# Value chunks that make their operand sums in place, half by half, with their weights loaded one quarter per step

## The chip, the cores and the metric

The kernel runs on one core of one Trainium2 chip. The core has five engines that run their own instruction streams: TensorE (PE in the profile; its weight loads are PEld), VectorE (DVE), ScalarE (ACT), GpSimd (POOL) and SyncE (SP). Each engine takes its instructions strictly in order; an instruction waits until what it reads is there and what it overwrites has been read. Transfers (DMA) between the chip's main memory and the on-chip memory are issued as instructions of SP or of ACT (rows SPq and ACTq) and then run on 16 DMA engines beside the compute engines.

The metric is the device time of one execution in microseconds, the median of the runs shown. The profile is of one execution.

## The reference, cut to what matters

The reference is one layer of a streaming encoder on 2048 rows of 1024 numbers. The rows are normed and multiplied by one wide weight matrix, whose columns are then split into queries, keys, values and gates of two branches and two mixing gates:

```python
IN_SPLITS = (A_WIDTH, A_WIDTH, A_WIDTH, A_WIDTH, R_QK_WIDTH, R_QK_WIDTH, R_V_WIDTH, R_V_WIDTH, D_MODEL, D_MODEL)
...
h = rms_norm(x, norm_gain[l])
proj = jnp.einsum('bsd,df->bsf', h, w_in[l])
q_a, k_a, v_a, g_a, q_r, k_r, v_r, g_r, m_a, m_r = split_columns(proj)
```

Branch A is attention over the own chunk of 64 rows and the eight before it, branch B a retention with a decaying state and a rotation of its queries and keys. Both are gated, projected, mixed and added to the input, and the sum is normed. The change concerns the projection `proj` alone, and of it the columns of the values `v_a` (512 columns) and `v_r` (1024 columns).

## The kernel before, in words

**Numbers.** All products are kept near fp32: an operand is split into a high part in fp32r (a cast by ScalarE, `wh`) and a low part, the rest (a subtraction by VectorE, `wl`), and a product is made of three matmuls: high by high, high by low, low by high.

**Strassen's scheme.** The big products are made in seven products of half-size blocks in place of eight. The seven left operands stay on the chip (the tiles `R[m]`, high and low). The right operands come from the weights of a chunk, four quarters b11, b12, b21, b22, and four sums made by GpSimd: t1 = b12 - b11, t2 = b22 - t1, t3 = b12 - b22, t4 = b21 - t2. The seven products use b11, t2, t3, b21, t1, t4 and b22 (the list `PRODUCTS`: left operand, right operand, PSUM bank).

**Chunks and steps.** The work of TensorE is one long list `seq` of items, walked by the generator `dense`. A projection job `p0` (rows 0 to 1023) or `p1` (rows 1024 to 2047) has eleven chunks: query, key, rotated key, value A, rotated query, first value B, key, rotated key, query, rotated query, second value B. Then come the gate jobs `g0`, `g1`, whose items are also used to fill TensorE during the attention and retention stages. An ordinary chunk (`Strassen`) has 256 columns and seven items of twelve matmuls with 512 columns each. A value chunk (class `Rows`: chunks 3, 5 and 10 of `p0` and `p1`) has 512 columns, and its result comes out with rows on the partitions. It has fourteen items, each of the seven products in two halves kk of the contraction, and its two halves of rows are two `Side` objects with their own PSUM banks. It takes its products in the order "g": b11, t2, b21, t3, t1, t4, b22.

**What sets the order.** The kernel writes the order of every engine by hand. While TensorE's item `at` is emitted, `prime` prepares the operand of item `at + 3` (`ahead[0]` is 3): `prepare` issues ScalarE's cast, and VectorE's low part is issued four steps later (`soon(LO_LAG, ...)`; an item is four steps). GpSimd's sums for an item are issued one preparation earlier still (`ch.sums`, called by `prime` for the item after the next one). For a value chunk, both halves of t1 and of t2 are issued together ahead of its first item's preparation, t3 and t4 ahead of the item that uses them. Evacuations of PSUM, stores and table loads are deferred by `later` and `put` to a later step, each on its engine's queue.

**Loads.** Weights are loaded by ScalarE's queue (`act.dma_start`). The dictionary `sooner` in `dense` says at which item a chunk's loads are issued: a lead of 9 and of 8 items before its first item (`RAW_LEADS`). The chunk behind a value chunk isn't loaded by these leads: at the value chunk's first item, `dense` sees that the following chunk has no weights yet and loads them then. An ordinary chunk has two tiles of 512 KB in a ring of three (tag "raw"). A value chunk loads b11 and b12 into two tiles of that ring at lead 9, and b21 and b22 as four transfers of 256 KB at lead 8 into four tiles of the general pool.

**Tiles.** The general pool of a projection phase (`E`, tag "e") has `E_PROJ` = 23 tiles of 2 KB per partition: casts and tables and results on their way to memory. A value chunk takes six of them: b21 and b22 in halves, and t2 in halves. Its t1 takes two of the three tiles of tag "t", t3 overwrites b12 and t4 overwrites b21.

**Start.** `start_up` norms and turns the first 1024 rows and makes the left operands of `p0` while the first two chunks (`Front`) run with plain products. It uses tiles of the general pool for x, for the turned blocks a11, a12 and a21, for the sum s3, and for two quarters of the second chunk's weights; s2 overwrites a11.

In the trace, buffer numbers are left out: `raw_p` are loaded quarters of `p0` and `p1` (also in the general pool, and after t3 or t4 has overwritten them), `t_p` are t1 to t4 in own tiles, `wh_p` and `wl_p` the high and low parts, `ps_p_x` to `ps_p_z` the PSUM banks. Nearly every instruction has line 142, the helper that records the order.

Of the kernel before, what the change touches and what calls it, by code (L numbers as in the profile page):

```python
# [11 lines left out]
F32 = mybir.dt.float32  # L12
# [4 lines left out]
ALU = mybir.AluOpType  # L17
# [4 lines left out]
P = 128  # L22
# [8 lines left out]
T = 256  # L31
# [12 lines left out]
ORDERS = {"p": (0, 4, 1, 2, 3, 5, 6), "g": (0, 1, 3, 2, 4, 5, 6)}  # L44
# [6 lines left out]
RAWS = 3  # L51
SUMS = 3
LO_LAG = 4
CS = 6
E_PROJ = 23
E_ATT = 16
E_RET = 22
E_MRG = 23
# [4 lines left out]
ROT_LATE = 10  # L63
PUT = 6
RAW_LEADS = (9, 8)
TR_LATER = 16
YR_0 = (2, 10, 1)
YR_1 = (102, 15, 2)
# [4 lines left out]
def hybrid_kernel(  # L73
# [23 lines left out]
    wp = ctx.enter_context(tc.tile_pool(name="wp", bufs=1))  # L97
# [4 lines left out]
    epool, xpool = [None], [None]  # L102

    def r32(ap):
        return ap.bitcast(F32)
# [7 lines left out]
    def E(name, dt=F32, shape=(P, 512)):  # L113
        return epool[0].tile(list(shape), dt, tag="e", name=name)
# [37 lines left out]
    pe, act, dve, pool = Ordered(nc.tensor), Sometimes(nc.scalar), Sometimes(nc.vector), Sometimes(nc.gpsimd)  # L152
# [107 lines left out]
    def soon(n, fn):  # L260

        later(n, fn) if ahead[0] else fn()
# [6 lines left out]
    class Chunk:  # L269
# [7 lines left out]
        def load(self, js=None):  # L277
            self.raw = self.raw or []
            for j in range(self.job.kh) if js is None else js:
                raw = wp.tile([P, 4, T], F32, tag="raw", bufs=RAWS, name=f"raw_{self.job.name}_{self.c}_{j}")  # L280
                (dma if self.job.resident else act.dma_start)(raw, self.job.stream(self.c, j))
                self.raw.append(raw)
# [36 lines left out]
    SUMS_OF = (("t1", "b12", "b11"), ("t2", "b22", "t1"), ("t3", "b12", "b22"), ("t4", "b21", "t2"))  # L319
# [14 lines left out]
    class Strassen(Chunk):  # L334
        tag = ""
# [32 lines left out]
        def prepare(self, n):  # L368
            self.sums(n)
            for s in SUMS_OF:  # L370
                if s[0] == PRODUCTS[n][1]:
                    self.sum(*s)
            late = pool if n in self.job.lo_pool else dve
            self.make(n, self.b[PRODUCTS[n][1]], late)
# [51 lines left out]
    class Rows(Strassen):  # L426
# [6 lines left out]

        def load(self, js=None):
            self.raw = self.raw or []
            for j in range(2) if js is None else js:
                for h in range(2):
                    src = w_cols(w_in, self.job.cols[self.c] + T * h, 2, j)
                    name = f"raw_{self.job.name}_{self.c}_{j}{h}"
                    if j == 0:  # L440
                        raw = wp.tile([P, 4, T], F32, tag="raw", bufs=RAWS, name=name)
                        act.dma_start(raw, src)
                        bs = [raw[:, 2 * kk:2 * kk + 2] for kk in range(2)]
                    else:
                        bs = [E(f"{name}_{kk}", shape=(P, 2, T)) for kk in range(2)]
                        for kk in range(2):
                            act.dma_start(bs[kk], src[:, 2 * kk:2 * kk + 2])
                    self.b[f"b{j + 1}{h + 1}"] = bs
                self.raw.append(j)

        def made(self, dst, one, two, into=None):
            if dst in self.b:
                return
            name = f"{dst}_{self.job.name}_{self.c}"
            if into:
                ts = self.b[into]
            elif dst == "t1":
                ts = [
                    wp.tile([P, 4, P], F32, tag="t", bufs=SUMS, name=f"{name}_{kk}")
                    .rearrange("p k c -> p (k c)").rearrange("p (k c) -> p k c", k=2)  # L460
                    for kk in range(2)
                ]
            else:
                ts = [E(f"{name}_{kk}", shape=(P, 2, T)) for kk in range(2)]
            for kk in range(2):
                pool.tensor_tensor(ts[kk], self.b[one][kk], self.b[two][kk], ALU.subtract)
            self.b[dst] = ts

        def sums(self, at):
            n, kk = at  # L470
            if kk:
                return
            if n == 0:
                self.made("t1", "b12", "b11")
                self.made("t2", "b22", "t1")
            elif n == 3:
                self.made("t3", "b12", "b22", "b12")
            elif n == 4:
                self.made("t4", "b21", "t2", "b21")

        def prepare(self, at):
            self.sums(at)
            n, kk = at
            src = self.b[PRODUCTS[n][1]][kk]
            name = f"{self.job.name}_{self.c}_{n}_{kk}"
            wh, wl = (
                wp.tile([P, 4, P], F32R, tag="p", bufs=PARTS, name=f"w{i}_{name}")
                .rearrange("p k c -> p (k c)").rearrange("p (k c) -> p k c", k=2)
                for i in "hl"
            )  # L490
            act.copy(wh, src)
            soon(LO_LAG, lambda: dve.tensor_tensor(wl, src, r32(wh), ALU.subtract))
            self.parts[at] = wh, wl

        def product(self, at):
            n, kk = at
# [120 lines left out]
    def dense(jobs):  # L617
        chunks = [ch for job in jobs for ch in job.chunks]
        following = dict(zip(chunks, chunks[1:]))
        starts = [k for k, (job, ch, n) in enumerate(seq) if isinstance(ch, Plain) and ch.at(n)[2] == 0]  # L620
        count, begins = {}, {}
        for at, (job, ch, n) in enumerate(seq):
            if isinstance(ch, Strassen):
                begins.setdefault(ch, at)
        sooner = {at - lead: (ch, [j]) for ch, at in begins.items() for j, lead in enumerate(RAW_LEADS)}
        one, two_, three = jobs[2].chunks[:3]
        for ch in (one, two_, three):
            for lead in RAW_LEADS:
                sooner.pop(begins[ch] - lead)
        two_.raw, three.raw = [], []  # L630
        at = begins[one]
        sooner[at - 9], sooner[at - 6] = (one, [0]), (one, [1])

        first_out = jobs[-1].chunks[0]
        at = begins[first_out]
        for lead in RAW_LEADS:
            sooner.pop(at - lead)
        sooner[at - 8], sooner[at - 5] = (first_out, [0]), (first_out, [1])
        operands = {begins[ch] - 2: ch for ch in begins if ch.job.before}
        for at, (job, ch, n) in enumerate(seq):  # L640
            free[0] = job.name[0] == "g"
            count[ch] = count.get(ch, 0) + 1
            if at in sooner:
                ch2, js = sooner[at]
                if ch2.raw is None or js[0]:
                    len(ch2.raw or ()) == js[0] and ch2.load(js)
            if count[ch] == job.when + 1 and ch in following and following[ch].raw is None:
                following[ch].load()
            prime(at + ahead[0] + 1)
            while starts and starts[0] <= at + job.lead:  # L650
                _, ch2, n2 = seq[starts.pop(0)]
                ch2.before(n2)
            if at in operands:
                operands[at].before()
            for _ in ch.product(n):
                yield True
                free[0] = job.name[0] == "g"
            for fn in hooks.get((job.name, ch.c, n), ()):
                fn()
            yield True  # L660
# [33 lines left out]
    def start_up():  # L694
# [3 lines left out]
        ch = jobs[0].chunks[:2]  # L698
# [5 lines left out]
        left, right = slice(0, P), slice(P, T)  # L704
# [45 lines left out]
                R[m][1][:, k, :], ps, ng[:, g:g + 1], r32(R[m][0][:, k, :]), ALU.mult, ALU.subtract  # L750
            )

        for i in range(2):
            ch[1].b[f"b2{i + 1}"] = E(f"b2{i + 1}", shape=(P, 4, P))
        for t in range(4):
            rows(xa, 0, t)
        for c in range(2):
# [32 lines left out]
        a11 = [E(f"a11_{k}") for k in range(4)]  # L790
# [14 lines left out]
        a12 = [E(f"a12_{k}") for k in range(4)]  # L805
# [16 lines left out]
                run_to(28)  # L822
        run_to(32)
        a21 = [E(f"a21_{k}") for k in range(4)]
        s3 = [E(f"s3_{k}") for k in range(4)]
        for k in range(4):
            act.activation(a21[k], ps[k], AF.Copy, scale=ng[:, k:k + 1])
            dve.scalar_tensor_tensor(s3[k], ps[k], ng[:, k:k + 1], a11[k], ALU.mult, ALU.subtract)
# [6 lines left out]
            hi(2, k, ps[k], 4 + k)  # L835
            lo(2, k, ps[k], 4 + k)
        run_to(48)
        s2, s1, s4 = a11, a21, a12
        for k in range(4):
            dve.scalar_tensor_tensor(s2[k], ps[k], ng[:, 4 + k:5 + k], s3[k], ALU.mult, ALU.add)  # L840
            pool.tensor_tensor(s4[k], a12[k], s2[k], ALU.subtract)
# [119 lines left out]
    def w_cols(w, col, n, j):  # L961
        rows = w.shape[1] // n
        return w[0, rows * j:rows * j + rows, col:col + T].rearrange("(k p) f -> p k f", p=P)
# [855 lines left out]

    st = open_phase("proj0", E_PROJ, 4)  # L1820
    jobs = [
# [15 lines left out]
    end, at = {}, 0  # L1837
# [65 lines left out]

    run_to(end["p0"] + TR_LATER + 4)
    flush()
# [6 lines left out]

    st = open_phase("proj1", E_PROJ, 4)
    ch = jobs[2].chunks[1]
    ch.b = {}
    for key in ("b11", "b12", "b21", "b22"):
        ch.b[key] = E(f"{key}_p1", shape=(P, 4, P))
        j, h = int(key[1]) - 1, int(key[2]) - 1
        dma(ch.b[key], w_cols(w_in, jobs[2].cols[1], 2, j)[:, :, h * P:(h + 1) * P])
    run_to(end["g0"])  # L1920
    for h in range(HEADS):
        later(10 + 44 * h, lambda h=h: finish_yr(h, 0, None, 18))
    run_to(end["p1"] + TR_LATER + 4)
    flush()
# [77 lines left out]
```

## Time and profile before

| what | before |
|---|---|
| median of 3 runs | 1956.41 us (1955.98 to 1958.45) |
| time of the profiled execution | 1955.38 us |
| its span | 1953.6 us |
| TensorE busy | 1887.9 us (97% of the span) |
| VectorE, GpSimd, ScalarE busy | 1373.3, 976.3, 931.4 us |
| mean granted TensorE clock | 0.996 |
| first matmul of the six value chunks | 92.1, 154.6, 286.0, 825.7, 886.8, 1013.9 us |

The span runs from the first to the last instruction of the profiled execution; a little time lies around it, 1955.38 - 1953.6 = 1.8 us here. Busy times are added over the instructions of an engine. A timeline row has the start and length in us, the engine, the operation, output<-inputs, the count where several instructions are merged, and in brackets the idle time of the engine before it with what ended it. The last row of the table is read off TensorE's timeline. The window views give the busy time per engine in a stretch, and the granted clock of TensorE as a share of full speed.

### The profile page before, as it was taken

Reading aid. Unit: us, or ns where it says so; the run is one execution under the profiler, and the core shown is the slowest. Engines: PE = TensorE matmul, PEld = TensorE weight load, DVE = VectorE, ACT = ScalarE, POOL = GpSimd, SP = SyncE. Lnnn points to the kernel's source line nnn. Section 1 sums busy time; section 2 is a strip of 40 time slices with the busy share of each in tenths; the row PEclk is TensorE's granted clock in tenths of the full one; section 3 lists DMA queues with packets and bytes.
Section 4 is the critical chain, followed back from the end, with each engine's and each line's share of the span. In section 5 each row is a group of like instructions: output and inputs, shape, how many; then the busy total and the mean of one; then the engine's idle time right before and its main releaser. Section 6 shows DMA issues by size and latency. Waiting matters only on the chain. (4 is left out here: it accounts for less than half of the span.)

```text
span 1953.6 us, 31951 instructions
## 1 busy us (share of the span) xinstructions
PE 1887.9 (97%) x10424; PEld 1617.1 (83%) x10424; DVE 1373.3 (70%) x2552; ACT 931.4 (48%) x1925; POOL 976.3 (50%) x795
## 2 busy tenths in 40 slices
PE   7999989999999999999999999999999999999997
PEld 6799879888888887799879888888888878887886
DVE  6978788677755658878787677765455655548876
ACT  7445554566654555343333565654455321223454
POOL 0534545555545565544445544554555114557775
PEclk9999999999999999999999999999999999999999
DMA  6575986656549988676675545544999999987564
GB/s 192 158 256 192 281 274 197 173 157 173 155 141 277 283 241 284 194 243 197 202 248 176 161 148 169 154 144 142 261 272 275 315 359 329 319 270 234 204 226 141
DMA packets 323317, 430.69 MB, mean 220 GB/s; under 512 B 30720, under 2 KB 190992, under 8 KB 323152
## 3 DMA queue, kind: packets, MB, share of 16 engines
q1 hardware_dynamic: 257216, 364.15, 58.5%
q10 hardware_dynamic: 65936, 64.50, 10.9%
q8 instruction: 83, 1.36, 0.3%
q14 instruction: 82, 0.67, 0.1%
HBM read 283.95 MB, written 144.59 MB: 219 GB/s over the span
## 5 line engine op out<-in xcount | busy, mean ns | idle before, releaser
L142 POOL TENSOR_SCALAR pr<-pr,rsum 128x640 f32<-128x640 f32 (+4 forms) x128 | 96.1, 751 | 218.0 <-DVE rsum L142 104.9
L142 PE MATMUL ps_g_z<-r,wh_g 128*128 128x512 f32 x448 | 143.8, 402 | 1.9 <-DVE c_g L142 1.9
L142 PE MATMUL ps_g_x<-r,wh_g 128*128 128x512 f32 x448 | 143.6, 402 | 1.0 <-ACT u_g L142 0.9
L142 DVE CUSTOM_DVE_ANT_0 pr<-wide,bt 128x640 f32<-128x640 f32 (+4 forms) x128 | 94.2, 736 | 67.7 <-PE wide L142 59.0
L142 ACT ACTIVATE pr<-pr,mn 128x640 f32<-128x640 f32 (+4 forms) x128 | 98.0, 766 | 80.8 <-DVE mn L142 80.8
L142 DVE TENSOR_TENSOR ptl<-tp,pth 128x384 fp32r<-128x384 f32 x168 | 95.8, 572 | 41.2 <-ACT pth L142 40.6
L142 ACT CAST pth<-tp 128x384 fp32r<-128x384 f32 x168 | 84.6, 516 | 70.6 <-PE tp L142 65.7
L142 POOL TENSOR_TENSOR sl<-sm,sh 128x384 fp32r<-128x384 f32 x64 | 69.0, 1077 | 63.2 <-ACT sh L142 44.3
L142 ACT CAST wh_p<-raw_p 128x512 fp32r<-128x512 f32 x99 | 61.4, 620 | 77.8 <-PE ps_p_v L142 31.4
L142 POOL TENSOR_TENSOR wl_g<-t_g,wh_g 128x512 fp32r<-128x512 f32 x56 | 75.6, 1350 | 39.4 <-ACT wh_g L142 38.1
L142 PE MATMUL wide<-ka,qa 128*128 128x512 f32 (+2 forms) x448 | 92.4, 322 | 2.1 <-DVE mn L142 2.0
L142 PEld LDWEIGHTS tp<-ident,pr 128*128 128x128 f32 x560 | 71.2, 141 | 27.9 <-POOL pr L142 2.8
L142 POOL TENSOR_TENSOR t_p<-raw_p,t_p 128x512 f32<-128x512 f32 x38 | 60.1, 1588 | 67.0 <-DVE wl_p L142 52.8
L142 PE MATMUL po<-pth,va 128*128 128x256 f32 x336 | 92.9, 297 | 0.0
L142 DVE TENSOR_TENSOR sm<-sr,dm 128x384 f32<-128x384 f32 x64 | 35.6, 556 | 81.1 <-PE sr L142 27.9
L142 PE MATMUL tp<-ident,pr 128*128 128x128 f32 x560 | 89.4, 273 | 2.9 <-POOL pr L142 1.6
L142 DVE TENSOR_TENSOR wl_p<-raw_p,wh_p 128x512 fp32r<-128x512 f32 x99 | 89.0, 908 | 4.5 <-ACT wh_p L142 4.4
L142 PEld LDWEIGHTS wide<-ka,qa 128*128 128x128 f32 x448 | 75.2, 189 | 20.3 <-DVE mn L142 8.2
L142 PE MATMUL po<-ptl,va 128*128 128x256 f32 x336 | 88.5, 285 | 2.2 <-DVE ptl L142 1.0
L142 PE MATMUL ps_g_z<-r,wl_g 128*128 128x512 f32 x224 | 88.1, 393 | 0.0
L142 PE MATMUL ps_g_x<-r,wl_g 128*128 128x512 f32 x224 | 88.1, 393 | 0.0
L142 DVE TENSOR_TENSOR wl_p<-t_p,wh_p 128x512 fp32r<-128x512 f32 x80 | 72.3, 906 | 22.1 <-ACT wh_p L142 22.1
(917 smaller groups left out, 6325.1 us busy)
## 6 DMA issues: line engine op xcount, KB each, us to landing
raw_g<-in_w_in_dram ACTq DMA_DIRECT2D x56, 512.0 KB, 4.9
raw_p<-in_w_in_dram ACTq DMA_DIRECT2D x38, 512.0 KB, 5.6
qa<-qas SPq DMA_DIRECT2D x128, 128.0 KB, 2.8
qr<-qrs SPq DMA_DIRECT2D x128, 128.0 KB, 4.8
vr<-vrs SPq DMA_DIRECT2D x64, 256.0 KB, 5.5
ka<-kas SPq DMA_DIRECT2D x40, 256.0 KB, 3.3
va<-vas SPq DMA_DIRECT2D x40, 256.0 KB, 2.9
kds<-kdt_k SPq DMA_DIRECT2D x32, 256.0 KB, 2.7
```

The costliest lines, as they stand in the source:

```text
L142: return tc.keep_in_program_order(op(*a, **k))
```

## The change

Six edits, all on the value chunks or on what makes room for them:

1. A value chunk's four quarters are loaded as four transfers of 512 KB, b12, b11, b22, b21, at leads 8, 7, 6 and 5, one per item (`ROW_LEADS`). b11 and b12 go to the ring of three as before; b21 and b22 go to a new tag "late" of two tiles of 4 KB.
2. The chunk behind a value chunk is no longer loaded at the value chunk's first item, but at leads 9 and 8 like other chunks.
3. t1 overwrites b11, and t2 takes two tiles of tag "t". t3 and t4 overwrite b12 and b21 as before.
4. The sums are made one half at a time, behind the preparation of an item (`SUMS_AFTER`; the number is that of the item among the fourteen): t1 and t2 of the first half behind item 1, of the second half behind item 2, t3 behind items 3 and 4, t4 behind items 6 and 7. `Rows.sums` does nothing.
5. The general pool of the projection phases has 19 tiles in place of 23.
6. In `start_up`, the two quarters of the second chunk's weights go to one tile of tag "late", s3 overwrites a11, and s2 gets tiles of its own.

```diff
-E_PROJ = 23
+E_PROJ = 19
...
+ROW_LEADS = (8, 7, 6, 5)
...
         def load(self, js=None):
             self.raw = self.raw or []
-            for j in range(2) if js is None else js:
-                for h in range(2):
-                    src = w_cols(w_in, self.job.cols[self.c] + T * h, 2, j)
-                    name = f"raw_{self.job.name}_{self.c}_{j}{h}"
-                    if j == 0:
-                        raw = wp.tile([P, 4, T], F32, tag="raw", bufs=RAWS, name=name)
-                        act.dma_start(raw, src)
-                        bs = [raw[:, 2 * kk:2 * kk + 2] for kk in range(2)]
-                    else:
-                        bs = [E(f"{name}_{kk}", shape=(P, 2, T)) for kk in range(2)]
-                        for kk in range(2):
-                            act.dma_start(bs[kk], src[:, 2 * kk:2 * kk + 2])
-                    self.b[f"b{j + 1}{h + 1}"] = bs
-                self.raw.append(j)
...
+            for j in range(4) if js is None else js:
+                k, h = ((0, 1), (0, 0), (1, 1), (1, 0))[j]
+                name = f"raw_{self.job.name}_{self.c}_{k}{h}"
+                if k:
+                    raw = epool[0].tile([P, 4, T], F32, tag="late", bufs=2, name=name)
+                else:
+                    raw = wp.tile([P, 4, T], F32, tag="raw", bufs=RAWS, name=name)
+                act.dma_start(raw, w_cols(w_in, self.job.cols[self.c] + T * h, 2, k))
+                self.b[f"b{k + 1}{h + 1}"] = [raw[:, 2 * kk:2 * kk + 2] for kk in range(2)]
+                self.raw.append(raw)
+
+        SUMS_AFTER = {1: ("t1", "t2", 0), 2: ("t1", "t2", 1), 3: ("t3", 0), 4: ("t3", 1), 6: ("t4", 0), 7: ("t4", 1)}
+
+        def made(self, dst, kk):
+            one, two = {s[0]: s[1:] for s in SUMS_OF}[dst]
+            into = {"t1": "b11", "t3": "b12", "t4": "b21"}
+            if dst == "t2":
+                t = wp.tile([P, 4, P], F32, tag="t", bufs=SUMS, name=f"t2_{self.job.name}_{self.c}_{kk}")
+                t = t.rearrange("p k c -> p (k c)").rearrange("p (k c) -> p k c", k=2)
             else:
...
+                t = self.b[into[dst]][kk]
+            pool.tensor_tensor(t, self.b[one][kk], self.b[two][kk], ALU.subtract)
+            self.b.setdefault(dst, []).append(t)
 
         def sums(self, at):
-            n, kk = at
-            if kk:
-                return
-            if n == 0:
-                self.made("t1", "b12", "b11")
-                self.made("t2", "b22", "t1")
-            elif n == 3:
-                self.made("t3", "b12", "b22", "b12")
-            elif n == 4:
-                self.made("t4", "b21", "t2", "b21")
+            pass
...
             soon(LO_LAG, lambda: dve.tensor_tensor(wl, src, r32(wh), ALU.subtract))
             self.parts[at] = wh, wl
+            *dsts, half = self.SUMS_AFTER.get(2 * ORDERS["g"].index(n) + kk, (0,))
+            for dst in dsts:
+                self.made(dst, half)
...
-        sooner = {at - lead: (ch, [j]) for ch, at in begins.items() for j, lead in enumerate(RAW_LEADS)}
+        sooner = {at - lead: (ch, [j]) for ch, at in begins.items()
+                  for j, lead in enumerate(ROW_LEADS if isinstance(ch, Rows) else RAW_LEADS)}
...
-            if count[ch] == job.when + 1 and ch in following and following[ch].raw is None:
+            if count[ch] == job.when + 1 and ch in following and following[ch].raw is None and not isinstance(ch, Rows):
                 following[ch].load()
...
-        for i in range(2):
-            ch[1].b[f"b2{i + 1}"] = E(f"b2{i + 1}", shape=(P, 4, P))
+        lower = epool[0].tile([P, 4, T], F32, tag="late", bufs=2, name="lower")
+        ch[1].b.update({"b21": lower[:, :, left], "b22": lower[:, :, right]})
...
-        s3 = [E(f"s3_{k}") for k in range(4)]
+        s3 = a11
...
-        s2, s1, s4 = a11, a21, a12
+        s2, s1, s4 = [E(f"s2_{k}") for k in range(4)], a21, a12
```

More of the change, by code (lines that the diff above doesn't have):

```diff
@@ L451, in made @@
-        def made(self, dst, one, two, into=None):
-            if dst in self.b:
-                return
[L454 to L462, printed above, removed]
-            else:
[L464 to L467, printed above, removed]
+            for j in range(4) if js is None else js:
[8 more added lines that the diff above has]
+                self.raw.append(raw)
@@ L469, in sums @@
         def sums(self, at):
-            n, kk = at
-            if kk:
-                return
-            if n == 0:
-                self.made("t1", "b12", "b11")
-                self.made("t2", "b22", "t1")
-            elif n == 3:
-                self.made("t3", "b12", "b22", "b12")
-            elif n == 4:
-                self.made("t4", "b21", "t2", "b21")
+            pass
         def prepare(self, at):
-            self.sums(at)
             n, kk = at
```

## The prediction

> **What bounds the kernel now.** I read the page's busy table first.
>
> ```profile
> span 1953.6 us, 31951 instructions
> PE 1887.9 (97%) x10424; PEld 1617.1 (83%) x10424; DVE 1373.3 (70%) x2552; ACT 931.4 (48%) x1925; POOL 976.3 (50%) x795
> ```
>
> TensorE works in 97% of the span, and the change takes no matmul away. It can win only where PE stands still: 1953.6 - 1887.9 = 65.7 us in all, or where PE runs at a lower clock. So the second view was PE's timeline, for its gaps, and the third the windows around them. Three places lie beside a load of a value chunk's weights:
>
> ```profile
> 79.97 0.50 PE L142 MATMUL ps_p_v<-r,wl_p 128*128 128x512 f32 x1 [3.42 <-DVE wl_p L142]
> ...
> 270.06 0.73 PE L142 MATMUL ps_p_y<-r,wh_p 128*128 128x512 f32 x2 [2.23 <-ACT wh_p L142]
> 275.45 0.50 PE L142 MATMUL ps_p_v<-r,wl_p 128*128 128x512 f32 x1 [1.56 <-DVE wl_p L142]
> ...
> 998.24 0.73 PE L142 MATMUL ps_p_y<-r,wh_p 128*128 128x512 f32 x2 [2.35 <-ACT wh_p L142]
> ```
>
> ```profile
> 75.00:80.00 5.00, 1.58 (x8) 0.97 (x6) 5.00 (x4) 1.51 (x3) 5.00 (x4) 1.00 0.91 249
> 80.00:85.00 5.00, 5.00 (x15) 3.98 (x16) 4.09 (x5) 1.76 (x5) 1.06 (x1) 0.66 0.87 247
> 85.00:90.00 5.00, 5.00 (x24) 4.14 (x23) 3.08 (x5) 1.12 (x3) 0.00 (x0) 1.00 0.01 4
> 265.00:270.00 5.00, 2.83 (x13) 2.02 (x11) 0.00 (x0) 0.61 (x2) 0.00 (x0) 1.00 1.06 370
> 270.00:275.00 5.00, 3.77 (x14) 2.48 (x14) 4.89 (x7) 4.76 (x12) 3.21 (x2) 1.00 1.02 346
> 995.00:1000.00 5.00, 2.65 (x9) 1.57 (x9) 1.78 (x4) 2.43 (x7) 0.96 (x1) 0.93 1.09 383
> 1000.00:1005.00 5.00, 5.00 (x17) 3.92 (x17) 5.00 (x7) 2.46 (x6) 3.77 (x4) 0.73 1.07 387
> ```
>
> The windows' columns are PE, PEld, DVE, ACT and POOL busy, granted clock, DMA share, GB/s. PE stands for 3.42, 2.23 + 1.56 = 3.79 and 2.35 us. After the first and the last gap the granted clock is low: 0.66 over 5 us costs 5 x 0.34 = 1.7 us (15 matmuls in that window, 24 in the next), and 0.93 then 0.73 cost 5 x 0.07 + 5 x 0.27 = 1.7 us. The middle pair kept 1.00. Together 3.42 + 1.7 + 3.79 + 2.35 + 1.7 = 13.0 us.
>
> Why does PE stand there? ScalarE's timeline at the three places:
>
> ```profile
> 66.53 4.04 ACTq L142 DMA_DIRECT2D raw_p<-in_w_in_dram  x3
> 70.66 0.59 ACT L142 CAST h_ka<-ps_p_(1, 1)_892 128x512 fp32r<-128x512 f32 x1 [3.57 <-PE ps_p_x L142]
> ...
> 255.71 0.42 ACTq L142 DMA_DIRECT2D raw_p<-in_w_in_dram  x1
> 258.85 0.38 ACTq L142 DMA_DIRECT2D raw_p<-in_w_in_dram  x1
> 260.64 8.71 ACTq L142 DMA_DIRECT2D raw_p<-in_w_in_dram  x4
> 269.39 0.62 ACT L142 CAST wh_p<-t_p 128x512 fp32r<-128x512 f32 x1 [8.32 <-DMA cs<-xs]
> ...
> 992.62 4.90 ACTq L142 DMA_DIRECT2D raw_p<-in_w_in_dram  x4
> 997.57 0.62 ACT L142 CAST wh_p<-t_p 128x512 fp32r<-128x512 f32 x1 [6.62 <-DMA raw_p<-in_w_in_dram]
> ```
>
> A value chunk's two lower quarters are loaded as four transfers issued in a row by ScalarE, right behind two larger ones. An issue is an instruction of ScalarE's queue, so a load that must wait holds the casts behind it: 8.71 us at 260.64, 4.90 us at 992.62. What it waits for is an earlier transfer's landing, at 269.39 one of the SP queue's stores (cs<-xs).
>
> **The change, part by part.**
>
> Loads. Two issues of 512 KB at lead 9 and four of 256 KB at lead 8 become four of 512 KB at leads 8, 7, 6, 5, one per step; b21 and b22 go to two buffers of their own. Bytes are the same; twelve issues fewer over six chunks cost nothing either way, ScalarE being busy 48% of the span. What goes is the burst.
>
> At the first place I take the whole of it. The chain is ScalarE's cast of 70.66, held 3.57 us, then VectorE behind it, which also works beside GpSimd's operand sums:
>
> ```profile
> 69.16 1.28 DVE L142 TENSOR_TENSOR r<-a,r 128x512 fp32r<-128x512 f32 x2
> 72.49 5.76 DVE L142 TENSOR_TENSOR r<-a,r 128x512 fp32r<-128x512 f32 x4
> 78.17 3.44 DVE L142 TENSOR_TENSOR wl_p<-t_p,wh_p 128x512 fp32r<-128x512 f32 x2
> ...
> 74.28 3.41 POOL L142 TENSOR_TENSOR t_p<-raw_p,t_p 128x512 f32<-128x512 f32 x2
> 77.66 3.40 POOL L142 TENSOR_TENSOR raw_p<-raw_p,raw_p 128x512 f32<-128x512 f32 x2
> ```
>
> Four subtractions take 5.76 us, where two took 1.28 just before: 3.2 us are lost beside GpSimd. Both causes leave this place, the loads by one to three steps and the sums by more than ten microseconds (they are made at leads 2 to 0, then later). Either alone is about the 3.42 us, so the gap and its clock go: -5.1 us (bounds 0 and -5.1).
>
> At the second and third place the DMA engines are full (share 1.06 at 370 GB/s, 1.09 at 383 GB/s), and the same bytes must still come. Spread over four steps, each load meets a queue that has had a step of some 2.7 us to drain, but not an empty one. Bounds: 0 and -3.79; 0 and -2.35 - 1.7 = -4.05. I take two thirds and three quarters, since three loads out of four no longer stand right behind another: -2.5 and -3.0 us. What is late next in ScalarE's queue if they still wait: the same casts of the chunk before.
>
> Loads of the chunk behind a value chunk move from its first step (lead 14) to leads 9 and 8. A 512 KB load lands in 5.6 us,
>
> ```profile
> raw_p<-in_w_in_dram ACTq DMA_DIRECT2D x38, 512.0 KB, 5.6
> ```
>
> which is two steps; the sums that need it come three steps on. Hidden: 0, up to 1 us a chunk if DMA is full.
>
> Sums in place. As many subtractions as before (eight a chunk, all on GpSimd), but when they run changes, and this is the cost. Before, t1 and t2 were ready at lead 5, four steps ahead of their cast. Now half a t1 overwrites b11 only after VectorE has made the low part of that half, then t2's half follows, and ScalarE's cast of it is next in its queue. The clean example is the second value chunk of the second projection, whose matmuls begin at 886.83:
>
> ```profile
> 881.46 0.68 DVE L142 TENSOR_TENSOR wl_p<-raw_p,wh_p 128x512 fp32r<-128x512 f32 x1
> 884.91 1.43 DVE L142 TENSOR_TENSOR wl_p<-raw_p,wh_p 128x512 fp32r<-128x512 f32 x1
> 890.12 0.69 DVE L142 TENSOR_TENSOR wl_p<-t_p,wh_p 128x512 fp32r<-128x512 f32 x1
> ...
> 884.12 0.62 ACT L142 CAST wh_p<-t_p 128x512 fp32r<-128x512 f32 x1 [1.43 <-POOL yr L142]
> 886.85 0.62 ACT L142 CAST wh_p<-t_p 128x512 fp32r<-128x512 f32 x1 [2.11 <-PE ps_p_z L142]
> ...
> 881.62 1.68 POOL L142 TENSOR_TENSOR yr<-yr,rb 128x512 f32<-128x512 f32 x1 [1.69 <-DVE yr L142]
> 893.34 2.83 POOL L142 TENSOR_TENSOR raw_p<-raw_p,t_p 128x512 f32<-128x512 f32 x1 [7.54 <-issue]
> ...
> 892.70 0.28 PE L142 MATMUL ps_p_y<-wl_p,r 128*128 128x256 f32 x1
> ```
>
> ```profile
> L142 DVE TENSOR_TENSOR wl_p<-raw_p,wh_p x99: 669/682/1793, 61.1 to 1046.4; 128x512 fp32r<-128x512 f32 x99
> L142 POOL TENSOR_TENSOR t_p<-raw_p,t_p x38: 1284/1624/1785, 59.3 to 1004.5; 128x512 f32<-128x512 f32 x38
> L142 POOL TENSOR_TENSOR t_p<-raw_p,raw_p x25: 1274/1352/1741, 60.9 to 1001.6; 128x512 f32<-128x512 f32 x25
> ```
>
> GpSimd is free at 881.62 + 1.68 = 883.3. With the medians, t1's first half ends at 884.65 and t2's at 886.27, so the cast of 884.12 waits 2.2 us. The second half can start when the low part of 884.91 is done (886.34): t1 to 887.7, t2 to 889.3, so the cast of 886.85 waits 2.4 us. Behind it in ScalarE's queue stand casts of the chunk before; PE needs the first of them at 892.70, over 8 us after its old place, so ScalarE's waits alone cost 0.
>
> VectorE is the tighter one. Its low part of t2's first half ends at 890.81 and PE reads it at 892.70: 1.9 us of room. GpSimd, idle here until 893.34, now runs three to four subtractions in this stretch. Beside one, a subtraction of VectorE takes up to 1793 ns in place of 682: 1.1 us more. Four would cost 4.4 us and leave PE 4.4 - 1.9 = 2.5 us short; none delayed costs 0. That VectorE isn't always the loser is seen at 893.34, where GpSimd's took 2.83 us. Bounds per chunk: 0 and +2.5. I take 0.6, nearer the low end, since two of the six chunks have GpSimd work in this stretch already and live with it: six chunks, +3.5 us.
>
> [...]
>
> Tiles. The general pool shrinks from 23 to 19 of 2 KB, and value chunks take none of it (six before: four loads, two t2). While such a chunk is in flight the others have two more. At the start they have fewer: with sixteen x tiles and four of a11 a wait appears at the second query tile, which must wait for the first one's store:
>
> ```profile
> 37.52 0.69 DVE L142 SCALAR_TENSOR_TENSOR l_qa<-ps_p_(0, 1)_594,h_qa 128x512 fp32r<-128x512 f32 x1 [2.03 <-ACT h_qa L142]
> 42.02 0.69 DVE L142 TENSOR_TENSOR l_ka<-ps_p_(0, 0)_659,h_ka 128x512 fp32r<-128x512 f32 x1 [2.50 <-ACT h_ka L142]
> ```
>
> Up to 1 us, and VectorE is idle 2.50 us soon after: 0. ScalarE's new waits at the last value chunk of the first projection meet a stretch full of its row scalings, which PE's transposes wait for: +0.5 us (0 to +2).
>
> Sum: -5.1 - 2.5 - 3.0 + 3.5 + 0.5 = -6.6 us. The profiled execution's own time is 1955.38 us, 1.0 under the median of the three runs, 1956.41; on the median the forecast is **1949.8 us**, its own range 1946 to 1953.
>
> **The rivals.**
>
> [...]
>
> [...]
>
> *The loads still wait.* DMA is the limit at 260 and 992 us, and its landings, not the burst, set when ScalarE goes on. Only the first place is won: -5.1 + 3.5 = -1.6, 1954.8 us, no change that can be told. For it: 370 to 383 GB/s at a share of 1.06 and more. Against: at 70 us the wait is of the same kind at a share near 1.
>
> *Starts cost nothing.* GpSimd loses, all 13.0 us come: 1943.4 us. For it: 2.83 us at 893.34. Against: 1.43 at 884.91.
>
> **How the numbers follow.** Forecast 0.52, slow starts 0.14, loads still wait 0.20, starts free 0.14. A measurement of this kernel tells about 0.2%, 3.9 us, from no change. Faster by more: nearly all of the forecast and the free starts, 0.50 + 0.14 = 0.64; same 0.24; slower 0.12. The range 1943 to 1958 holds the forecast, the free starts and the waiting loads, 0.86 less their tails.
>
> **What would show it.** Loads right: no ACTq row of a value chunk over some 2 us, no PE gap of over 1 us near 77, 268 and 996 us, and a granted clock of 1.00 near 80. Sums right: ScalarE's casts of t2 wait for GpSimd, and PE shows gaps on DVE wl at the third item of value chunks, small ones. Wrong: those gaps reach 2 us and the clock falls behind them, or the long ACTq rows remain.

## The result, and the profile after

The changed kernel takes 1962.42 us, the median of 21 runs (1957.01 to 1970.35). The kernel before took 1956.41 us in 21 runs beside it (1947.38 to 1961.35). The ratio is 1.0035, with a 95% interval of 1.0025 to 1.0046: slower by 0.35%, 6.0 us. The forecast was 1949.8 us. The profiled execution of the changed kernel took 1958.73 us, near the low end of its runs, so the two traces differ by less than the medians: their spans are 1956.6 and 1953.6 us, 3.0 us apart. Of all the executions that this text rests on, one is left out of every median and ratio: 2651.32 us at a mean granted clock of 0.656, in the last kernel of the experiments.

The page's first lines of the changed kernel:

```profile
span 1956.6 us, 31952 instructions
PE 1892.4 (97%) x10424; PEld 1621.9 (83%) x10424; DVE 1381.7 (71%) x2552; ACT 930.1 (48%) x1925; POOL 970.1 (50%) x795
```

**The gaps at the three load places are gone.** The windows of the changed kernel there (PE, PEld, DVE, ACT, POOL busy, granted clock, DMA share, GB/s), and two of ScalarE's casts behind a load's issue, with the idle time of ScalarE before them:

```profile
75.00:80.00 5.00, 5.00 (x24) 4.14 (x23) 3.18 (x5) 3.47 (x8) 0.00 (x0) 1.00 0.89 263
80.00:85.00 5.00, 5.00 (x24) 4.14 (x23) 3.26 (x4) 1.37 (x4) 1.53 (x2) 1.00 1.10 329
265.00:270.00 5.00, 5.00 (x24) 4.11 (x23) 4.82 (x10) 2.57 (x6) 1.53 (x1) 1.00 1.08 370
1000.00:1005.00 5.00, 5.00 (x24) 4.14 (x23) 4.30 (x9) 2.71 (x6) 0.00 (x0) 1.00 1.09 382
```

```profile
271.62 0.62 ACT L143 CAST wh_p<-t_p 128x512 fp32r<-128x512 f32 x1 [2.06 <-DMA raw_p<-in_w_in_dram]
...
815.89 0.62 ACT L143 CAST wh_p<-t_p 128x512 fp32r<-128x512 f32 x1 [6.31 <-DMA raw_p<-in_w_in_dram]
```

PE is busy 5.00 of 5.00 us in each, at a clock of 1.00, where it stood 2 to 3.4 us before. The DMA engines are as full as they were (370 and 382 GB/s, as in the windows of before). The issues now stand 2.7 to 3.8 us apart near 265 us, and the longest wait of ScalarE behind one there is 2.06 us, where the row of four held a cast for 8.32 us. The waits are not gone, though: ScalarE still waits 6.31 us behind an issue at 815 us, and 5.37 us near 145 us. TensorE has no gap of over 0.2 us there, so these waits cost nothing.

**The starts of the value chunks took it back.** TensorE's timeline of the changed kernel, its new gaps of more than 0.6 us up to 1030 us:

```profile
90.33 0.39 PE L143 MATMUL ps_p_x<-wl_p,r 128*128 128x256 f32 x1 [0.70 <-DVE wl_p L143]
...
107.36 0.33 PE L143 MATMUL trkr_k<-ident,u_p 128*128 128x128 f32 x1 [0.87 <-DVE u_p L143]
109.96 0.39 PE L143 MATMUL ps_p_v<-wl_p,r 128*128 128x256 f32 x1 [1.94 <-DVE wl_p L143]
...
160.81 0.39 PE L143 MATMUL ps_p_y<-wl_p,r 128*128 128x256 f32 x1 [0.81 <-DVE wl_p L143]
...
832.92 0.39 PE L143 MATMUL ps_p_y<-wl_p,r 128*128 128x256 f32 x1 [2.30 <-DVE wl_p L143]
...
897.75 0.38 PE L143 MATMUL ps_p_y<-wl_p,r 128*128 128x256 f32 x1 [1.93 <-DVE wl_p L143]
...
1023.54 0.39 PE L143 MATMUL ps_p_y<-wl_p,r 128*128 128x256 f32 x1 [2.92 <-DVE wl_p L143]
```

Five of the seven wait for a low part of a value chunk at its third item (bank y: t2's first half) or seventh (bank v: t3's first half). The others wait for a low part at the second item (90.33) and for a key (107.36). Together the seven are 11.5 us. Behind three of them the clock falls; the windows there:

```profile
110.00:115.00 5.00, 5.00 (x30) 5.00 (x31) 4.09 (x8) 2.00 (x6) 1.28 (x1) 0.66 1.04 369
830.00:835.00 5.00, 2.70 (x21) 2.50 (x20) 5.00 (x7) 2.15 (x6) 3.11 (x3) 0.94 0.32 108
835.00:840.00 5.00, 5.00 (x34) 5.00 (x33) 4.96 (x6) 1.95 (x6) 2.97 (x3) 0.72 0.30 105
895.00:900.00 5.00, 3.07 (x23) 2.87 (x23) 5.00 (x8) 2.81 (x6) 1.54 (x1) 0.92 0.15 52
900.00:905.00 5.00, 5.00 (x34) 5.00 (x34) 4.97 (x8) 1.06 (x2) 2.20 (x2) 0.74 0.89 278
```

Each fall costs 1.7 us: 5 x 0.34; 5 x 0.06 + 5 x 0.28; 5 x 0.08 + 5 x 0.26. So the starts cost 11.5 + 5.1 = 16.6 us and the load places give the 13.0 us of the prediction's sum: 3.6 worked out, 3.0 measured. The agreement is a net one. Elsewhere the trace of the changed kernel has three more falls of the clock (near 260, 757 and 1797 us) where that of before has one (985 us), 3 x 1.7 - 1.7 = 3.4 us, and its other gaps of over 0.3 us add up to 40.5 us in place of 43.9, 3.4 us less.

**Where VectorE's time goes.** VectorE's timeline around the first value chunk of the second projection, whose first matmul is at 825.7 us before and at 824.6 us after. Before:

```profile
824.43 0.69 DVE L142 TENSOR_TENSOR t_k<-c_p,cs_k 128x512 f32<-128x512 f32 x1
825.03 0.69 DVE L142 TENSOR_TENSOR t_k<-u_p,cs_k 128x512 f32<-128x512 f32 x1
825.75 0.69 DVE L142 TENSOR_TENSOR u_p<-u_p,cs_k 128x512 f32<-128x512 f32 x1
826.48 0.69 DVE L142 TENSOR_TENSOR u_p<-u_p,t_k 128x512 f32<-128x512 f32 x1
827.09 0.68 DVE L142 TENSOR_TENSOR u_p<-ps_p_z,u_p 128x512 f32<-128x512 f32 x1
827.69 0.68 DVE L142 TENSOR_TENSOR c_p<-c_p,cs_k 128x512 f32<-128x512 f32 x1
828.29 1.78 DVE L142 TENSOR_TENSOR wl_p<-t_p,wh_p 128x512 fp32r<-128x512 f32 x1
```

After, VectorE and then GpSimd:

```profile
823.69 0.68 DVE L143 TENSOR_TENSOR t_k<-c_p,cs_k 128x512 f32<-128x512 f32 x1
824.29 1.78 DVE L143 TENSOR_TENSOR t_k<-u_p,cs_k 128x512 f32<-128x512 f32 x1
826.10 1.67 DVE L143 TENSOR_TENSOR u_p<-u_p,cs_k 128x512 f32<-128x512 f32 x1
827.81 1.67 DVE L143 TENSOR_TENSOR u_p<-u_p,t_k 128x512 f32<-128x512 f32 x1
829.40 0.68 DVE L143 TENSOR_TENSOR u_p<-ps_p_z,u_p 128x512 f32<-128x512 f32 x1
830.00 1.19 DVE L143 TENSOR_TENSOR c_p<-c_p,cs_k 128x512 f32<-128x512 f32 x1
831.12 1.75 DVE L143 TENSOR_TENSOR wl_p<-t_p,wh_p 128x512 fp32r<-128x512 f32 x1
...
823.85 1.68 POOL L143 TENSOR_TENSOR raw_p<-raw_p,raw_p 128x512 f32<-128x512 f32 x1 [0.63 <-DVE wl_p L143]
825.60 1.62 POOL L143 TENSOR_TENSOR t_p<-raw_p,raw_p 128x512 f32<-128x512 f32 x1
827.18 3.46 POOL L143 TENSOR_TENSOR raw_p<-raw_p,raw_p 128x512 f32<-128x512 f32 x2
```

The same six operations ahead of the low part take 828.29 - 824.43 = 3.9 us before and 831.12 - 823.69 = 7.4 us after. They rotate the keys of the chunk before and have nothing to do with the sums; no row has a bracket, so VectorE waits for no operand. GpSimd's four subtractions (t1 and t2 of the second half, both halves of t3) stand beside the slowed ones. The row at 829.40 reads PSUM and takes 0.68 us although GpSimd works. The whole trace of the changed kernel says the same. Take VectorE's two-input operations (TENSOR_TENSOR) of 128x512. Of 190 with both inputs in SBUF, the on-chip memory, that began while one of GpSimd's had over 0.3 us to go, 182 took over 0.9 us; of the 468 others none did. Of 118 that began so with an input in PSUM none took over 0.69 us. Before, GpSimd made the same sums at 811 to 824 us, ahead of this stretch, where VectorE still has pauses (2.95 us up to 815.06), and stood idle from 823.9 to 827.9 us.

The gap of 2.30 us can be added up from this. Before, the low part ended at 828.29 + 1.78 = 830.07 us and TensorE read it at 831.61: 1.5 us of room. After, it ends at 831.12 + 1.75 = 832.87, 2.8 us later, and TensorE, ahead since the load gaps are gone, wants it at 830.6, 1.0 us sooner: 2.8 + 1.0 - 1.5 = 2.3 us.

The lengthening is up to 1.1 us here, less than one of GpSimd's subtractions of 1.62 to 1.73 us, and the operation with a PSUM input has none. No run shows what the two engines share.

### The profile page after: what moved, and what is told of

It is laid out like the page before. It is cut to its first block, busy times and chain, and to the rows that moved or that the text cites. A ratio compares the mean times of both kernels' runs of the same rounds, so it can differ in the third digit from the quotient of the medians.

```text
span 1956.6 us, 31952 instructions
## 1 busy us (share of the span) xinstructions
PE 1892.4 (97%) x10424; PEld 1621.9 (83%) x10424; DVE 1381.7 (71%) x2552; ACT 930.1 (48%) x1925; POOL 970.1 (50%) x795
## 5 line engine op out<-in xcount | busy, mean ns | idle before, releaser
L143 DVE TENSOR_TENSOR wl_p<-raw_p,wh_p 128x512 fp32r<-128x512 f32 x111 | 93.1, 849 | 6.5 <-ACT wh_p L143 6.4
L143 ACT CAST wh_p<-raw_p 128x512 fp32r<-128x512 f32 x111 | 68.0, 618 | 55.3 <-PE ps_p_v L143 16.4
L143 POOL TENSOR_TENSOR t_g<-raw_g,t_g 128x512 f32<-128x512 f32 x56 | 74.2, 1324 | 26.3 <-DVE wl_g L143 9.8
L143 PEld LDWEIGHTS ps_g_z<-r,wh_g 128*128 128x128 f32 x448 | 76.2, 191 | 10.4 <-issue 2.3
```

Source lines behind the costliest of these rows:

```text
L143: return tc.keep_in_program_order(op(*a, **k))
```

## The experiments

Theory A: the sums' new place costs the time, since VectorE loses time beside GpSimd's subtractions (up to 1.1 us an operation) in a stretch where it has no slack, and the loads' gain is real. The rivals are B (the load gaps went because the sums left those places), C (the starts are late for another reason), D (the chain from b11's low part over t1, t2 and the cast is late by itself) and E (VectorE has too much work at the starts, whoever runs beside it). All ratios are to runs of the kernel before on the same chip; they are worked out from all runs and differ from the quotient of two medians by up to 0.0009.

| kernel | loads | t1, t2, t3 | median us | ratio (95%) |
|---|---|---|---|---|
| before | old | early, GpSimd | 1956.4 | 1 |
| early sums | new | early, GpSimd | 1949.5 | 0.9957 (0.9940 to 0.9974) |
| sums only | old | in place, GpSimd | 1972.3 | 1.0074 (1.0057 to 1.0091) |
| after | new | in place, GpSimd | 1962.4 | 1.0035 (1.0025 to 1.0046) |
| sums only, VectorE | old | in place, VectorE | 1957.8 | 1.0008 (0.9994 to 1.0021) |
| sums on VectorE | new | in place, VectorE | 1947.3 | 0.9953 (0.9935 to 0.9970) |
| all sums on VectorE | new | in place, VectorE, t4 too | 1945.5 | 0.9937 (0.9922 to 0.9952) |
| early, t3 on VectorE | new | early; t3 VectorE | 1943.6 | 0.9939 (0.9918 to 0.9959) |
| no sums | new | left out | 1944.3 | 0.9935 (0.9922 to 0.9949) |

**Early sums.** The loads of the change, the sums where they stood in the program before it.

```diff
-            *dsts, half = self.SUMS_AFTER.get(2 * ORDERS["g"].index(n) + kk, (0,))
-            for dst in dsts:
-                self.made(dst, half)
+            self.sums(at)
```

> The loads as in the changed kernel; t1 and t2 in tiles of their own and whole at lead 5, t3 and t4 as before the change. [...] Rival B (the load gaps went because the sums left those places, not because of the loads): the gap near 77 us comes back with its low clock, some 5 us, and parts of the others: 1948 to 1955 us. Rival C (the starts are late for another reason, the new load order or the smaller pool): 1958 to 1962 us.

Theory A has the start gaps gone and the load gaps away, 1956.4 - 14 = 1942 us. Measured: 1949.5 us, ratio 0.9957. Faster than both kernels, and the three load gaps stay away. Near 270 and 998 us GpSimd's sums are back (t1 begins at 266.31 and 998.26 us, before at 273.14 and 999.04), so B falls there. Near 77 us this run doesn't test B: with b22 loaded later, t2 and t3 begin at 81.88 and 84.85 us there, where they began at 74.28 and 77.66. But the time isn't 1942: its timeline shows gaps at starts that neither the forecast nor theory A had,

```profile
91.52 0.39 PE L143 MATMUL ps_p_x<-wl_p,r 128*128 128x256 f32 x1 [1.64 <-DVE wl_p L143]
...
828.98 0.39 PE L143 MATMUL ps_p_y<-wl_p,r 128*128 128x256 f32 x1 [1.59 <-DVE wl_p L143]
...
1013.19 0.38 PE L143 MATMUL ps_p_y<-wl_p,r 128*128 128x256 f32 x1 [1.39 <-DVE wl_p L143]
```

4.6 us in all. The same sums now lie closer to the chunk's start: near 90 and 1010 us t1 begins 12.1 and 7.5 us ahead of the chunk's first matmul, where it began 21.8 and 14.8 us ahead before.

**Sums only.** The converse: the sums of the change with the old loads. (The later load of the chunk behind was kept.) Against the kernel before:

```diff
-            self.sums(at)
...
+            *dsts, half = self.SUMS_AFTER.get(2 * ORDERS["g"].index(n) + kk, (0,))
+            for dst in dsts:
+                self.made(dst, half)
```

> The kernel before, with its loads of value chunks (leads 9 and 8, four of 256 KB in a row) and 23 tiles, but with the sums half by half in place and the chunk behind loaded at leads 9 and 8. Theory A: the starts cost as in the changed kernel, about +17 us, the gaps near 270 and 998 us stay, the one near 77 us shrinks since its sums are gone: 1966 to 1973 us. Rival B: with the sums moved the load gaps go too, 1958 to 1962 us.

Measured: 1972.3 us, as theory A has it. The rows of four issues are as long as they were (9.40 us near 263 us, 4.35 near 1005), so it is the loads that hold ScalarE. The gap near 77 us is gone all the same: there it was enough to take the sums away. At the second place 1.26 + 0.49 = 1.75 of the 3.79 us stay, near 1010 us all and more (4.36 us). The two effects add: 0.9957 x 1.0074 = 1.0031, and both together measured 1.0035.

**t3 later.** In the changed kernel t3 is made behind t4's first half.

```diff
-        SUMS_AFTER = {..., 3: ("t3", 0), 4: ("t3", 1), 6: ("t4", 0), 7: ("t4", 1)}
+        SUMS_AFTER = {..., 5: ("t4", "t3", 0), 6: ("t3", 1), 7: ("t4", 1)}
```

> The changed kernel with t3's two halves made behind t4's first half, so about 8 us later. Theory A: two of six subtractions of GpSimd leave the stretch in which VectorE falls behind, each cost VectorE 1.0 to 1.1 us; the start gaps of 1.9 to 2.9 us shrink to under 1 us, over five starts with their clock about -8 us: 1954 us. Rival D (the chain b11's low part, t1, t2, cast, low part is what is late, whatever runs beside it): the start gaps stay as they are, 1962 us. Both: a later cast of t3 could give a small gap at the seventh item.

Measured: 1961.0 us, ratio 1.0014 (1.0000 to 1.0028). By the ratios it is 4 us faster than the changed kernel, half of what theory A expected. The timeline says more:

```profile
835.53 0.39 PE L143 MATMUL ps_p_y<-wl_p,r 128*128 128x256 f32 x1 [0.84 <-DVE wl_p L143]
850.70 0.50 PE L143 MATMUL ps_p_v<-wl_p,r 128*128 128x256 f32 x1 [1.87 <-DVE wl_p L143]
901.21 0.39 PE L143 MATMUL ps_p_y<-wl_p,r 128*128 128x256 f32 x1 [0.46 <-DVE wl_p L143]
914.16 0.39 PE L143 MATMUL ps_p_v<-wl_p,r 128*128 128x256 f32 x1 [1.18 <-DVE wl_p L143]
...
1024.97 0.39 PE L143 MATMUL ps_p_y<-wl_p,r 128*128 128x256 f32 x1 [0.94 <-DVE wl_p L143]
1037.92 0.39 PE L143 MATMUL ps_p_v<-wl_p,r 128*128 128x256 f32 x1 [1.10 <-DVE wl_p L143]
```

At the third item 2.30, 1.93 and 2.92 us become 0.84, 0.46 and 0.94, though the chain of t1 and t2 is untouched: D falls. New gaps of 1.1 to 1.9 us stand at the seventh item, which uses t3. Most of the debt was moved, not paid.

**No sums.** All eight subtractions are left out: an operand stands in for each sum, and the output is not the reference's.

```diff
-            pool.tensor_tensor(t, self.b[one][kk], self.b[two][kk], ALU.subtract)
-            self.b.setdefault(dst, []).append(t)
+            self.b.setdefault(dst, []).append(self.b[two][kk])
```

> The changed kernel with all eight subtractions of a value chunk left out (b11 stands for t1 and t2, b22 for t3, b11 for t4; the output is not the reference's). Theory A: VectorE's subtractions at the starts take 0.68 us again, no start gap over 0.5 us, 1940 us or a little less than with early sums. If the starts' gaps stay, VectorE's own list there is too long and theory A falls: 1958 us or more.

Measured: 1944.3 us, and at the value chunks no gap over 0.4 us that waits for a low part. VectorE's own list is therefore not too long, and C has nothing left to explain.

**Sums on VectorE.** The test that parts A from E: the busier engine takes over the work, six subtractions of 0.68 us, 4.1 us a chunk.

```diff
-            pool.tensor_tensor(t, self.b[one][kk], self.b[two][kk], ALU.subtract)
+            eng = pool if dst == "t4" else dve
+            eng.tensor_tensor(t, self.b[one][kk], self.b[two][kk], ALU.subtract)
```

> The changed kernel with t1, t2 and t3 subtracted by VectorE in place of GpSimd, at the same places of the program (t4 stays on GpSimd). [...] Rival E (VectorE simply has too much work at the starts, and GpSimd hides the sums): 4.1 us more at each of six starts, 1975 us or more.

Measured: 1947.3 us, ratio 0.9953; against the changed kernel 0.9953 / 1.0035 = 0.9918, 16 us. E falls. Theory A, by which the 4.1 us are about what VectorE lost beside GpSimd while t1 and t2 come sooner, has 1956 to 1962 us, and missed by 9 us: VectorE also makes a sum in 0.69 us where GpSimd takes 1.3 to 1.7, so t2 is ready sooner, and no run tells apart how much of the 16 us is that and how much is VectorE's loss beside GpSimd. VectorE's timeline at the same start as above:

```profile
820.15 0.69 DVE L143 TENSOR_TENSOR t_k<-c_p,cs_k 128x512 f32<-128x512 f32 x1
820.75 0.69 DVE L143 TENSOR_TENSOR raw_p<-raw_p,raw_p 128x512 f32<-128x512 f32 x1
821.48 0.69 DVE L143 TENSOR_TENSOR t_p<-raw_p,raw_p 128x512 f32<-128x512 f32 x1
822.09 0.69 DVE L143 TENSOR_TENSOR t_k<-u_p,cs_k 128x512 f32<-128x512 f32 x1
822.81 0.69 DVE L143 TENSOR_TENSOR u_p<-u_p,cs_k 128x512 f32<-128x512 f32 x1
...
824.74 0.68 DVE L143 TENSOR_TENSOR c_p<-c_p,cs_k 128x512 f32<-128x512 f32 x1
825.34 1.78 DVE L143 TENSOR_TENSOR wl_p<-t_p,wh_p 128x512 fp32r<-128x512 f32 x1
```

Eight operations, two of them sums, take 825.34 - 820.15 = 5.2 us, where six took 7.4 us beside GpSimd. Against the 3.9 us before, a sum costs VectorE (5.2 - 3.9) / 2 = 0.65 us if it makes it, and (7.4 - 3.9) / 4 = 0.9 us if GpSimd does.

Moving the sums from GpSimd to VectorE won 16 us here, and 13 us with the old loads (the next run beside sums only, 1.0008 / 1.0074).

**Sums only, VectorE.** The same edit with the old loads.

> The kernel with the sums alone (loads as before the change), with t1, t2 and t3 subtracted by VectorE. Theory A: what VectorE's own subtractions win is independent of the loads: as in the changed kernel some 15 us, 1972.3 - 15 = 1957 us; against the changed kernel with VectorE's sums (1947.3) it then shows the loads once more, about 10 us. If the loads were worth nothing: 1947 us.

Measured: 1957.8 us. The loads are worth 0.9953 / 1.0008 = 0.9945 here, 10.8 us.

**Two other load orders.** b22 loaded first, with t3 right behind t1 and t2, and with t3 where the early sums have it.

```diff
-                k, h = ((0, 1), (0, 0), (1, 1), (1, 0))[j]
+                k, h = ((1, 1), (0, 1), (0, 0), (1, 0))[j]
```

> The kernel with early sums, but b22 loaded first of the four quarters (then b12, b11, b21) and t3 made right behind t1 and t2. Theory A: the six subtractions end some 2 to 4 us earlier, before VectorE's dense stretch at the chunk's first matmul; the start gaps that the early sums still have (1.6, 1.6 and 1.4 us near 91, 829 and 1013 us) shrink to under 0.7 us: some -4 us against the early sums' 1949.5, 1945 to 1947 us. If the gaps stay, what is left at the starts isn't GpSimd's place: 1949 to 1950 us.

> As the run before it with t3 where the early sums have it. Since GpSimd takes its next subtraction as soon as its operands are there, t3's place in the program matters only where another instruction of GpSimd's queue stands ahead: the same time as with t3 early within 1 us, 1945 to 1948 us under theory A; 1949 to 1950 us otherwise.

Measured: 1958.7 us (ratio 1.0006, 0.9991 to 1.0021) and 1958.5 us (0.9998, 0.9983 to 1.0012). The edit did the opposite of what was meant. t1 needs b11, which now comes third. GpSimd's timeline of the second kernel, and TensorE's:

```profile
82.41 2.55 POOL L143 TENSOR_TENSOR t_p<-raw_p,raw_p 128x512 f32<-128x512 f32 x2 [17.69 <-DMA raw_p<-in_w_in_dram]
...
1010.47 3.00 POOL L143 TENSOR_TENSOR t_p<-raw_p,raw_p 128x512 f32<-128x512 f32 x2 [12.13 <-DMA raw_p<-in_w_in_dram]
...
94.37 0.58 PE L143 MATMUL ps_p_x<-wl_p,r 128*128 128x256 f32 x1 [3.55 <-DVE wl_p L143]
...
1023.78 0.39 PE L143 MATMUL ps_p_y<-wl_p,r 128*128 128x256 f32 x1 [3.57 <-DVE wl_p L143]
```

With the early sums t1 began at 74.62 and 998.26 us. It now begins 7.8 and 12.2 us later by the clock on the wall, 6.8 and 3.8 us later against the chunk's first matmul, and the gaps of 1.64 and 1.39 us grow to 3.55 and 3.57. As a dose this speaks for A; as a better version it failed. That t3's place in the program doesn't matter came true (0.2 us by the medians; the ratios' intervals overlap).

**The chunk behind, loaded at the first item again** (early sums otherwise).

```diff
-... and following[ch].raw is None and not isinstance(ch, Rows):
+... and following[ch].raw is None:
```

> The kernel with early sums, but the chunk behind a value chunk is loaded at the value chunk's first item, as before the change. The prediction put the later load at 0, up to 1 us a chunk: 1949.5 us, or 1947 if the later load had cost up to 1 us at some of them. If two loads at the first item held ScalarE, it would be slower: 1952 us or more.

Measured: 1951.1 us, ratio 0.9975 (0.9961 to 0.9989), beside 0.9957 (0.9940 to 0.9974). The ratios are 3.5 us apart, in favour of the later load, but the intervals overlap.

**Which version is best?** Three more, by the engine line alone: t4 on VectorE too; early sums with t3 on VectorE; early sums with t3 and t4 on VectorE.

> The changed kernel with all four sums, t4 too, subtracted by VectorE. t4's two subtractions lie in the middle of a chunk, where VectorE has more slack, and cost it there 2 x 0.68 in place of up to 1.1 lost beside GpSimd: within 2 us of the 1947.3 with t4 on GpSimd.

> The kernel with early sums, with t3 alone subtracted by VectorE. Of the two slowed operations that t3 costs VectorE at the starts (1.1 us each) 2 x (1.1 - 0.68) = 0.8 us a chunk come back, and GpSimd is done with its four subtractions some 3.5 us earlier: start gaps of 1.4 to 1.6 us under 1 us, 1945 to 1948 us. [...]

> The kernel with early sums, with t3 and t4 subtracted by VectorE, t1 and t2 early on GpSimd. Moving t4 too won 1.8 us when all sums stood in place (1947.3 to 1945.5), on chips that may differ; if that adds to the early sums with t3 on VectorE (1943.6), 1942 us; if t4's place has slack and its price is nothing, 1943.6 again within 1.5 us.

Measured: 1945.5 us (0.9937), 1943.6 us (0.9939), 1947.0 us (0.9954, 0.9939 to 0.9969). By the ratios the first two beat the kernel before by some 12 us and the changed kernel by some 19 us, and they can't be told apart, nor from the kernel without any sums (0.9935). What is late next is a row scaling of ScalarE: near 280 us TensorE waits 2.58 us for it in the second, 2.23 us in the kernel without sums, where the early sums wait 0.86 us. The third missed its expectation, which was at or under the second; the intervals of the two overlap, and its profiled execution (1944.1 us) shows no new gap at a value chunk. Why it is no faster stays open.

## Why the prediction was wrong, point by point

- **Load gaps** (-5.1, -2.5, -3.0): all three went wholly, where two thirds and three quarters of the second and third were forecast. By the places of the same matmuls in the two traces, from ahead of the gap to the end of the low clock, PE gained 5.3, 4.7 and 4.5 us. In whole runs the loads gave 0.9957 (8.4 us), 1.0035 / 1.0074 (7.6 us) and 10.8 us in three settings. The 10.6 us of the sum is at the upper end of that; the discount for full DMA engines wasn't needed at the places themselves, and what the whole runs with early sums lack of the 13.0 us is the 4.6 us of new start gaps.
- **First place, either cause alone:** shown for the sums, by sums only. For the loads it isn't shown, since in early sums t2 and t3 had moved there too.
- **Chunk behind** (0): not told from 0.
- **Tiles** (0): right. The rows of the start's query and key tiles are the same in the changed kernel: 2.03 and 2.49 us of idle time, against 2.03 and 2.50.
- **ScalarE at the last value chunk of the first projection** (+0.5): PE loses 0.9 us there, by the places of the same matmuls on both sides of the four transposes near 286 us. The 892.70 us that the prediction gives as PE's need of a cast is the row of t2's low part, but that ScalarE's waits cost nothing at the starts held: none of the new gaps waits for ScalarE.
- **Starts of value chunks** (+3.5): **this step failed.** Its bounds were 0 and +2.5 us a chunk, and it took 0.6, "nearer the low end, since two of the six chunks have GpSimd work in this stretch already and live with it". Measured: 0.70 + 0.87 + 1.94, 0.81, none, 2.30, 1.93 and 2.92 us, together 11.5 us, and three falls of the clock, 5.1 us: 16.6 us, 2.8 a chunk. In whole runs the sums' place costs 1.0074 (14.5 us) with the old loads and 1.0035 / 0.9957 = 1.0078 (15.3 us) with the new. The mechanism was the one named, down to the 1.1 us per operation and the third item. The size was wrong for three reasons. The row from which hope was taken, GpSimd's 2.83 us at 893.34, showed who loses once, not who loses in a row: at 824 us VectorE lost three times running, and 7.4 - 3.9 = 3.5 us of the 4.4 us of the upper bound. TensorE came sooner, by 1.0 us in that chunk, which the 1.9 us of room left out. And the low clock behind the gaps, 5.1 us, was not in the forecast's sum.
- **The rivals.** Slow starts, at a chance of 0.14, had this result in kind: 2.5 us short at each of six starts is 15.0 us of gaps (11.5 measured), a low clock behind half of them is 5.1 us (5.1 measured), and with the -10.6 of the loads that is +9.5, 1966 us (1962.4 measured). That the clock fell behind just three starts is luck in part, since the same pause can pass without a fall (last section). Waiting loads fell: the same GB/s, no gap, though ScalarE still waits up to 6.31 us behind an issue. Free starts fell.
- **What would show it wrong** was named rightly: gaps of 2 us at the third item and a low clock behind them.

## What to carry to other kernels

Before an instruction of GpSimd is moved, look at what VectorE does in the new stretch: here an operation of VectorE with two SBUF inputs (128x512, fp32) that began while one of GpSimd's was running took up to 1.1 us longer (182 of 190 took over 0.9 us in place of 0.68), and what counts is whether VectorE has slack there, not whether GpSimd has. If it has none, try the sum on the busy engine itself: 0.65 us of its own was cheaper than 0.9 us of waiting. And transfers that follow one another in a compute engine's queue are worth spreading one per step even where the DMA engines are full: 8 to 11 us here, although some of the waits stayed.

## What the runs showed of the hardware that was not expected

The same pause of TensorE is followed by a low clock in one trace and not in the other. Near 259 us both kernels wait for ScalarE twice (1.63 and 0.45 us before, 1.65 and 0.45 after). The windows behind it, before and then after:

```profile
260.00:265.00 5.00, 5.00 (x26) 4.11 (x25) 3.08 (x4) 1.07 (x2) 2.99 (x2) 1.00 1.03 344
```

```profile
260.00:265.00 5.00, 5.00 (x18) 3.91 (x19) 4.14 (x6) 3.72 (x9) 3.42 (x3) 0.66 0.90 260
```

And the longest start gap, 2.92 us at 1023.54, has a clock of 1.00 behind it, while 1.94 us at 109.96 (with 0.87 us shortly ahead of it) has 0.66:

```profile
1025.00:1030.00 5.00, 5.00 (x44) 5.00 (x44) 4.96 (x7) 2.46 (x5) 1.68 (x1) 1.00 0.46 161
```

Length alone doesn't decide, then; each fall shown costs 1.7 us (5 x 0.34 at 260 and at 110 us). What does decide isn't shown: no run here set the moment at which a pause falls, and 0.87 and 1.94 us with work between them were enough for a fall.
